# Another order of two transposings, and later places for small matmuls, in a two-branch mixer layer

## The chip, the cores and the metric

The kernel runs on one core of a Trainium2 chip. The metric is the device time of one execution in microseconds (us). TensorE does the matmuls, VectorE and ScalarE the elementwise work, GpSimd (Pool) the powers and some fills, and SyncE (SP) issues the DMAs. In the rows of the profile PE is TensorE's matmul, PEld its weight load, DVE is VectorE and ACT is ScalarE.

## The reference

Two layers run over 128 context tokens and 256 latent tokens, 384 rows of 2048 channels. In each, one input projection feeds two branches: A, a bidirectional RWKV-7 mixer with 16 heads of 64, and B, a bidirectional gated DeltaNet with 8 heads of 128 in chunks of 64 tokens. Both are projected back, merged by gates and projected once more. Of branch B this matters here:

```
lower = where(strict, einsum('nbhik,nbhjk->nbhij', kb, kc) * decay, 0)
t_inv = triangular_solve(eye + lower, eye, lower=True, unit_diagonal=True)
u  = t_inv @ (vc * beta)
wk = t_inv @ (kb * exp(gcum))
...                       # a scan over the chunks uses u, wk, q, k and the decays
```

Keys and queries are divided by their norms before, and the decays come from cumulative sums of g. Branch A has the same kind of inverse in its chunked form, and a norm of its own over k.

## The kernel before

The dense products (input projection, branch projections, merge, output projection) are streams of 128x128 weight tiles in float16, split from float32 on ScalarE (line 247) and VectorE (line 249) into a high and a low part; a product is 48 matmuls of 384 columns. They are one generator, `dense`. The branches are generators too, *threads*: `rwkv_front`, `rwkv_corner`, `rwkv_back` and `rwkv_out` for a pair of A's heads, `gdn_front`, `gdn_corner`, `gdn_scan` and `gdn_out` for a head of B (`gdn_corner` for two heads). `weave` sets TensorE's order once, when the program is written: it keeps a planned time, `now`, that each matmul advances. A thread yields either a number, the planned nanoseconds after which it wants to go on, or the name of an event that another thread sets. Whenever no thread is due, the products go on by one step (`STEP`, two tiles of the contraction, six matmuls). So the number that a thread yields between two matmuls says how much of the products TensorE gets to do between them. TensorE then keeps that order; it does not go past an instruction that waits. The other engines' orders are fixed as well, by a scheduler that works from the same program.

`HOP` (1100) is the allowance for one trip over another engine and back, `HOP_G` (4.4 of these) for a trip over VectorE, Pool and back, and `INVERT_A` and `INVERT_B` are those for an inverse in the two branches.

A head of branch B goes as follows. `gdn_front` builds `E` on VectorE, sums it by three matmuls with triangles (the decays), and takes the exponentials on ScalarE. It squares the keys (line 1280) and the queries (1290) on ScalarE and sums each by matmuls with `ones`; Pool takes the power (1299), and a matmul spreads the norms `rs`. The products of keys with keys and queries (`KQ`) follow, and VectorE and ScalarE write the masked, negated blocks into `nB`. After every second head `invert` inverts all 32x32 diagonal blocks of both heads on VectorE: a transposing into `ivw` (line 569), 30 steps of a multiply (574) and an add (576), and two transposings, `a1` in place of `nB` (580) and `a2` into the tile `iva` (581). `gdn_corner` waits for the event of the inverse, scales `a1` and `a2` into `Uf` on ScalarE (1351), and multiplies the corner block: a first product of `Ln` with `a2` (12 matmuls for a head, `tps<-iva,Ln` in the rows), a copy into `xc`, and a second product with `a1`. Then `gdn_scan` runs over the chunks. *Corner 1* to *corner 4* are the four pairs of heads in layer 0, *corner 5* to *corner 8* those in layer 1. Branch A's corners use the same `invert` (its results there are `nA` and `iva`) and also begin with `a2`.

At the start of branch B the products are held until head 0's front is done: the projections of head 2 wait for that event, and nothing else is left.

Of the kernel before, what the change touches and what calls it, by code (L numbers as in the profile page):

```python
# [27 lines left out]


HOP_G = 4.4  # L30
HOP, HOP_V, EVAC, CONV, DECAY, FIRST_B, INVERT_A, INVERT_B = 1100, 1.2, 2000, 8000, 7000, 3000, 37000, 48000

RANKS, STEP = (2000, 1000, 0, 0, 0, 0), 2

# [19 lines left out]
def backbone(ctx: ExitStack, tc: tile.TileContext, i, o):  # L54
    nc = tc.nc
    V, S, G, PE = nc.vector, nc.scalar, nc.gpsimd, nc.tensor
# [172 lines left out]
    def run(fast):  # L229
# [213 lines left out]
        def layer(l, par, cw, hpar, omka, xs, ready, next_start, after):  # L443
# [121 lines left out]
            def invert(pool, n_t):  # L565


                W = pool.tile([128, 32, 32], F32, tag="ivw", name="ivw", bufs=1)
                V.transpose(out=W, in_=n_t.rearrange("p b t -> p t b"))  # L569
                for j in range(1, 31):  # L570
                    n = 31 - j
                    tmp = pool.tile([128, 256], F32, tag="ivt", name="ivt", bufs=1)
                    tv = tmp[:, 0:n * j].rearrange("p (a b) -> p a b", b=j)
                    V.tensor_tensor(out=tv, in0=W[:, j + 1:32, j:j + 1].to_broadcast([128, n, j]),  # L574
                                    in1=W[:, j:j + 1, 0:j].to_broadcast([128, n, j]), op=MULT)
                    V.tensor_tensor(out=W[:, j + 1:32, 0:j], in0=W[:, j + 1:32, 0:j], in1=tv, op=ADD)  # L576
                G.memset(W.rearrange("p a b -> p (a b)")[:, 0:1024:33], 1.0)
                a1 = n_t
                a2 = pool.tile([128, 32, 32], F32, tag="iva", name="iva2", bufs=1)
                V.transpose(out=a1.rearrange("p b t -> p t b"), in_=W)  # L580
                V.transpose(out=a2.rearrange("p b s -> p s b"), in_=W.rearrange("p t s -> p s t"))  # L581
                return a1, a2


# [22 lines left out]
            for n in range(6):  # L607
                t = P.tile([128, 128], F32, tag=f"sring{n}", name=f"sring{n}", bufs=1)
# [37 lines left out]
            def rwkv_front(hp):  # L646
# [4 lines left out]
                k = act["k", hp]  # L651
                sq = P.tile([128, T], F32, tag="pe", name="sq", bufs=1)
                S.activation(out=sq, in_=k, func=AF.Square, scale=pcol(R_KK, hp))
                yield HOP
                t = tps()
                for b in range(NBLK):
                    mm(t[:, 2 * b:2 * b + 2], sq[:, 128 * b:128 * b + 128], bones[:, 0:128:64])
# [3 lines left out]
                t = tps()  # L661
# [12 lines left out]
                for d in range(2):  # L674
                    t = tps()
# [3 lines left out]
                    t = tps()  # L679
# [35 lines left out]
                    if d == 0:  # L715
                        yield "v", l, hp
                        v = act["v", hp]
                        t = tps()
# [16 lines left out]
                    for h in range(2):  # L735
                        for p in range(2):
                            t = tps()
# [10 lines left out]
                    for p in range(2):  # L748
                        t = tps()
# [8 lines left out]
                    t = tps()  # L758
# [488 lines left out]
            def gdn_front(h):  # L1247
# [11 lines left out]
                for n, (bm, d) in enumerate((("le", 0), ("lt", 1), ("ge", 1))):  # L1259
                    V.tensor_tensor(out=E[:, 3 * n:3 * n + 3, :], in0=half[bm].unsqueeze(1).to_broadcast([128, 3, 64]),  # L1260
                                    in1=bc(g[:, 8 * d + h, :], 64), op=MULT)
                yield 2 * HOP
                t = tps()
                mm(t[:, 0:192], tri["gt"], E[:, 0:3, :])
                mm(t[:, 192:384], tri["ge"], E[:, 3:6, :])
# [12 lines left out]
                ka = act["kb", h]  # L1278
                sq = Q.tile([128, T], F32, tag="th", name="sq", bufs=1)
                S.activation(out=sq, in_=ka, func=AF.Square)  # L1280
                yield HOP
                t = tps()
                for b in range(NBLK):
                    mm(t[:, b:b + 1], sq[:, 128 * b:128 * b + 128], ones[:, 0:1])
# [4 lines left out]
                sq = Q.tile([128, T], F32, tag="th", name="sq", bufs=1)  # L1289
                S.activation(out=sq, in_=qa, func=AF.Square)  # L1290
                S.copy(KQ[:, :, 1:3, :], c4(qa))
                yield HOP
                t = tps()
                for c in range(6):
                    b, p = divmod(c, 2)
# [1 line left out]
                with tc.high_priority(offset=1):  # L1297
                    V.tensor_scalar(out=rs[:, 3:6], in0=t[:, 0:3], scalar1=128.0, scalar2=128.0 * EPS, op0=MULT, op1=ADD)
                    G.tensor_tensor(out=rs, in0=rs, in1=mhalf[:, 0:6], op=ALU.pow)
                yield HOP_G * HOP  # L1300
                t = tps()
                for b in range(NBLK):
                    mm(t[:, 128 * b:128 * b + 128], rs[:, b:b + 1].to_broadcast([128, 128]), ident)
# [38 lines left out]
            def gdn_corner(h0):  # L1342
                yield "inverse", l, 8 + h0 // 2
                a1, a2 = act["inverse", h0 // 2]
                for hh in range(2):
                    Ln = act["front", h0 + hh][6]
                    i0 = 6 * hh
                    Uf = Q.tile([128, 2, NBLK, 64], F32, tag="Uf", name="Uf", bufs=4)
                    for q in range(2):
                        for d, a in ((0, a1), (1, a2)):  # L1350
                            S.mul(Uf[:, d, :, 32 * q:32 * q + 32], a[:, i0 + 3 * d:i0 + 3 * d + 3, :], m01[:, q:q + 1])
                    xc = Q.tile([128, 6, 32], F32, tag="xc", name="xc", bufs=2)
                    qs = [(slice(64 * p, 64 * p + 32), slice(64 * p + 32, 64 * p + 64)) for p in range(2)]
                    t = tps()
                    for n in range(6):
                        for q0, q1 in qs:
                            mm(t[q1, 32 * n:32 * n + 32], Ln[q0, n // 3, n % 3, 32:64], a2[q0, i0 + n, :])
                    for q0, q1 in qs:
                        S.copy(xc[q1].rearrange("p b c -> p (b c)"), t[q1, 0:192])
                    yield HOP  # L1360
                    t = tps()
                    for b in range(NBLK):
                        for q0, q1 in qs:
                            mm(t[q0, 32 * b:32 * b + 32], xc[q1, b, :], a1[q1, i0 + b, :])
                            mm(t[q1, 32 * b:32 * b + 32], a1[q1, i0 + 3 + b, :], xc[q1, 3 + b, :])
                    for q0, q1 in qs:
                        S.mul(Uf[q0, 0, :, 32:64], t[q0, 0:96].rearrange("p (b c) -> p b c", b=NBLK), -1.0)
                        S.mul(Uf[q1, 1, :, 0:32], t[q1, 0:96].rearrange("p (b c) -> p b c", b=NBLK), -1.0)
                    act["corner", h0 + hh] = Uf
                event(("corner", l, 8 + h0 // 2), HOP)  # L1370
# [178 lines left out]
    with tc.tile_pool(name="ck", bufs=1) as ck:  # L1549
# [14 lines left out]
        t = tps()  # L1564
# [33 lines left out]
```

## Time and profile before

| | |
|---|---|
| three runs, median | 3184.18 us (3180.49 to 3192.88) |
| the profiled execution | 3183.25 us, span 3180.3 us |
| granted TensorE clock, mean | 0.974 |
| TensorE matmul busy | 2991.0 us, 94% |
| TensorE weight loads | 1997.2 us, 63% |
| VectorE busy | 2310.9 us, 73% |
| ScalarE busy | 1455.9 us, 46% |

The span is what the profiler saw between the first and last instruction. Busy time is the sum of an engine's instructions over the whole span; branch A of layer 0 runs from some 140 to 950 us and its branch B to some 1460 us, those of layer 1 from 1670 to 2505 and to 2990 us. Granted clock is the share of TensorE's full clock: 1.0 is 2.4 GHz, 0.5 is 1.2 GHz, and there is no other level in the rows.

### The profile page before, as it was taken

What the parts mean: (1) busy time and instruction counts of PE and PEld (TensorE: products, weight loads), DVE (VectorE), ACT (ScalarE), POOL (GpSimd) and SP (SyncE); (2) the same over time, 40 slices, a digit from 0 to 9 for tenths busy, and PEclk for the clock granted to TensorE, in tenths of its full rate; (3) what the DMA queues carried; (4) which work ended last, traced back from release to release, by engine and by line L of the source; (5) the groups of instructions that cost most, each with busy time, mean ns of one, the idle gap of its engine ahead of it and who ended that gap; (6) DMA issues with size and microseconds to landing.
All of it is one profiled execution on the core that took longest, in us unless ns stands there. A gap on an engine that the chain in (4) does not pass through costs nothing. (4 is left out here: it accounts for less than half of the span.)

```text
span 3180.3 us, 69999 instructions
## 1 busy us (share of the span) xinstructions
PE 2991.0 (94%) x28531; PEld 1997.2 (63%) x28531; DVE 2310.9 (73%) x5968; ACT 1455.9 (46%) x3122; POOL 144.9 (5%) x198
## 2 busy tenths in 40 slices
PE   6899999999999999998979999999999998899898
PEld 2466666666665555555976666666666655565588
DVE  3268888888877777866354788888888678867744
ACT  3344444444434565453355444444443446564432
POOL 1000000011000000000000000000000000000000
PEclk8999999999999999999989999999999999999999
DMA  9854454454455436367455544433434442325655
GB/s 331 274 157 134 130 146 126 129 139 129 136 158 167 127 94 178 109 192 241 125 158 158 144 141 131 137 82 92 108 103 128 120 110 78 106 79 160 203 142 158
DMA packets 644359, 457.86 MB, mean 144 GB/s; under 512 B 28026, under 2 KB 611004, under 8 KB 642492
## 3 DMA queue, kind: packets, MB, share of 16 engines
q1 hardware_dynamic: 644028, 453.29, 49.1%
q8 instruction: 226, 3.70, 0.5%
q14 instruction: 105, 0.86, 0.1%
HBM read 421.74 MB, written 31.49 MB: 143 GB/s over the span
## 5 line engine op out<-in xcount | busy, mean ns | idle before, releaser
L95 PE MATMUL jps<-x,w 128*128 128x384 f16 x8640 | 1532.1, 330 | 10.1 <-ACT x L247 8.5
L95 PEld LDWEIGHTS <-w 128*128 128x128 f16 (+1 forms) x10368 | 975.9, 99 | 692.4 <-issue 100.6
L249 DVE SCALAR_TENSOR_TENSOR w<-st,w 128x1024 f16<-128x1024 f32 (+2 forms) x552 | 641.1, 1168 | 246.8 <-ACT w L247 241.9
L247 ACT ACTIVATE w<-st 128x1024 f16<-128x1024 f32 (+2 forms) x552 | 553.3, 1009 | 467.7 <-PE jps L95 304.5
L95 PE MATMUL cps<-w,mg 128*128 128x128 f16 x4608 | 263.6, 221 | 8.6 <-ACT mg L247 5.2
L95 PEld LDWEIGHTS <-mg 128*128 128x128 f16 x4608 | 262.0, 99 | 10.2 <-ACT mg L247 5.5
L576 DVE TENSOR_TENSOR ivw<-ivw,ivt 128x30 f32<-128x30 f32 (+4 forms) x720 | 236.6, 329 | 14.1
L574 DVE TENSOR_TENSOR ivt<-ivw 128x30 f32<-128x30 f32 (+4 forms) x720 | 236.6, 329 | 13.9
L95 PE MATMUL jps<-ya,w 128*128 128x384 f16 x768 | 137.7, 329 | 8.3 <-DVE z L562 2.9
L95 PEld LDWEIGHTS <-x 128*128 128x128 f16 x2304 | 132.3, 99 | 11.1 <-issue 7.9
L95 PE MATMUL jps<-w,x 128*128 128x128 f16 x2304 | 136.6, 220 | 0.0
L95 PE MATMUL tps<-AR,BK 64*128 64x128 f32 x768 | 121.6, 293 | 4.1 <-DVE GR L744 2.3
L95 PE MATMUL acc<-wm,cpad 128*32 128x256 f32 (+1 forms) x1664 | 112.0, 379 | 12.8 <-DMA wm<-in_w_mod 12.8
L757 ACT ACTIVATE nA<-GA 32x192 f32<-32x192 f32 x128 | 46.1, 360 | 152.7 <-DVE GA L742 151.7
L1400 ACT ACTIVATE os<-cps,gx 64x128 f32<-64x128 f32 x160 | 57.9, 362 | 117.6 <-DVE rt L1398 115.2
L95 PEld LDWEIGHTS tps<-AR,BK 64*128 64x128 f32 x768 | 97.0, 191 | 18.7 <-issue 4.3
L894 ACT COPY AR<-cps 64x128 f32<-64x128 f32 x192 | 49.5, 258 | 118.6 <-PE cps L95 104.9
L867 DVE COPY Z<-cps 64x128 f32<-64x128 f32 x192 | 55.4, 289 | 64.5 <-PE cps L95 60.8
L884 DVE SCALAR_TENSOR_TENSOR sring<-cps,pl,sp 64x64 f32<-64x64 f32 x256 | 72.5, 283 | 30.8 <-PE cps L95 26.5
L95 PEld LDWEIGHTS acc<-wm,cpad 128*32 128x32 f32 x1664 | 42.6, 110 | 61.4 <-issue 29.7
L1061 DVE TENSOR_TENSOR og<-cps,gp 128x128 f32<-128x128 f32 x96 | 27.6, 288 | 69.0 <-ACT junk L1060 69.0
L95 PE MATMUL jps<-yb,w 128*128 128x384 f16 x408 | 74.6, 329 | 1.4 <-ACT yb L247 1.3
(356 smaller groups left out, 3665.0 us busy)
## 6 DMA issues: line engine op xcount, KB each, us to landing
st<-in_w_in SPq DMA_DIRECT2D x194, 1024.0 KB
wm<-in_w_mod SPq DMA_DIRECT2D x176, 512.0 KB
st<-in_w_o SPq DMA_DIRECT2D x32, 1024.0 KB
st<-in_w_pa SPq DMA_DIRECT2D x32, 512.0 KB
gates<-gt SPq DMA_DIRECT2D x64, 192.0 KB
ms<-gates SPq DMA_DIRECT2D x32, 384.0 KB
st<-in_w_pb SPq DMA_DIRECT2D x11, 1024.0 KB
wm<-in_w_mod SPq DMA_DIRECT2D x32, 256.0 KB
```

Of the source, the lines that this page charges most:

```text
L95: PE.matmul(out, lhsT=lhsT, rhs=rhs, start=start, stop=stop, **kw)
L247: S.activation(out=dst[0], in_=src, func=AF.Copy, scale=scale)
L249: V.scalar_tensor_tensor(out=dst[1], in0=src, scalar=scale, in1=dst[0], op0=MULT, op1=SUB, accum_out=flag())
L574: V.tensor_tensor(out=tv, in0=W[:, j + 1:32, j:j + 1].to_broadcast([128, n, j]), in1=W[:, j:j + 1, 0:j].to_broadcast([128, n, j]), op=MULT)
L576: V.tensor_tensor(out=W[:, j + 1:32, 0:j], in0=W[:, j + 1:32, 0:j], in1=tv, op=ADD)
L757: S.mul(nA[rq, 6 * d:6 * d + 6, :].rearrange("p (h b) t -> p h b t", h=2), GA[rq, :, p, :, 32 * q:32 * q + 32], -1.0)
L867: V.tensor_copy(dirs[d][4][ar, b, p, :], pb[ar, 0:128])
L884: V.scalar_tensor_tensor(out=sn[hs, hs], in0=pb[hs, o0:o0 + 64], scalar=plc[hs], in1=sp[hs, hs], op0=MULT, op1=ADD)
L894: S.copy(AR[rr, b, 2 * p:2 * p + 2, :].rearrange("p a b -> p (a b)"), pas[d][rr, 0:128])
L1061: V.tensor_tensor(out=og[:, b, 128 * d:128 * d + 128], in0=t[:, 0:128], in1=gp[:, stream_of(b), 128 * d:128 * d + 128], op=MULT)
L1400: S.activation(out=os_[d][R_, b, :], in_=pas[d][R_, 0:128], func=AF.Copy, scale=egs[R_, x, b:b + 1])
```

## The change

In `invert` the two transposings change places: `a2`, which the corner's first product reads, is written first, `a1` second. `gdn_corner` scales `a2`'s half first. Five allowances grow: the inverse of branch B from 48000 to 52500, the squares of both branches (one in A, two in B) from 1 to 2.5 `HOP`, the norms of branch B from 4.4 to 6, and the decays from 2 to 3.5.

```diff
-HOP, HOP_V, ..., INVERT_A, INVERT_B = 1100, 1.2, ..., 37000, 48000
+HOP, HOP_V, ..., INVERT_A, INVERT_B = 1100, 1.2, ..., 37000, 52500
+HOP_S, HOP_N = 2.5, 6.0
...                                       invert
+V.transpose(out=a2.rearrange("p b s -> p s b"), in_=W.rearrange("p t s -> p s t"))
 V.transpose(out=a1.rearrange("p b t -> p t b"), in_=W)
-V.transpose(out=a2.rearrange("p b s -> p s b"), in_=W.rearrange("p t s -> p s t"))
...                                       rwkv_front, after the square of k
-yield HOP
+yield HOP_S * HOP
...                                       gdn_front, after E
-yield 2 * HOP
+yield 3.5 * HOP
...                                       gdn_front, after the squares of k and of q
-yield HOP
+yield HOP_S * HOP
...                                       gdn_front, after the power
-yield HOP_G * HOP
+yield HOP_N * HOP
...                                       gdn_corner
-for d, a in ((0, a1), (1, a2)):
+for d, a in ((1, a2), (0, a1)):
```

The changed file has two lines more at its head, so its line 97 is line 95 of before. Three places show what moves. First TensorE at a square of branch A, in layer 0 before head pair 4 (`w` are the parts of a weight tile, `x` of the input, and `bones` sums the squares); before:

```order
L95 LDWEIGHTS w_5546
L95 MATMUL jps<-x_198,w_5546 128x384
L95 MATMUL tps<-bones,sq 128x2 x3
L95 LDWEIGHTS w_5545
L95 MATMUL jps<-x_198,w_5545 128x384
```

and after:

```order
L97 MATMUL jps<-x_199,w_5545 128x384
L97 LDWEIGHTS w_5546
L97 MATMUL jps<-x_198,w_5546 128x384
L97 MATMUL tps<-bones,sq 128x2 x3
L97 LDWEIGHTS w_5545
L97 MATMUL jps<-x_198,w_5545 128x384
```

The three matmuls stand twelve rows later, behind six more products; so do all 16 squares of branch A. Second TensorE at the start of branch B in layer 1, where the products run out (`E` are the decays' sums, `sq` the squares of keys and queries, `rs` the norms, `p` the keys and values that are transposed); before:

```order
L95 LDWEIGHTS w_30107
L95 MATMUL jps<-x_19599,w_30107 128x384
L95 MATMUL tps<-ones,sq 128x1 x3
L95 MATMUL tps<-ones,sq 64x1 x6
L95 MATMUL tps<-ident,rs 128x128 x3
L104 MATMUL tps<-ident,p_29892 128x128 x3
L104 MATMUL tps<-ident,p_29658 128x128 x3
L95 MATMUL tps<-KQ 64x128 x6
```

and after:

```order
L97 LDWEIGHTS w_30107
L97 MATMUL jps<-x_19599,w_30107 128x384
L97 MATMUL tps<-E,m_gt 128x192
L97 MATMUL tps<-E,m_ge 128x192
L97 MATMUL tps<-E,m_lt 128x192
L97 MATMUL tps<-ones,sq 128x1 x3
L97 MATMUL tps<-ones,sq 64x1 x6
L97 MATMUL tps<-ident,rs 128x128 x3
L106 MATMUL tps<-ident,p_29892 128x128 x3
L106 MATMUL tps<-ident,p_29658 128x128 x3
L97 MATMUL tps<-KQ 64x128 x6
```

The last step of products has moved from behind the decays to ahead of them. Third VectorE at the end of corner 2's inverse (`ss` and `os` belong to a scan's output, `rt` to a scan's step, `vb` to the values); before:

```order
L574 TENSOR_TENSOR ivt<-ivw 128x30
L1314 TENSOR_TENSOR vb<-vtok,beta 128x384
L576 TENSOR_TENSOR ivw<-ivw,ivt 128x30
L1260 TENSOR_TENSOR E<-b_ge,g 128x192
L1398 SCALAR_TENSOR_TENSOR rt<-cps,neg,vtok 64x128
L1398 SCALAR_TENSOR_TENSOR rt<-cps,neg,vb 64x128
L580 STREAM_TRANSPOSE nB<-ivw 128x32x32
L581 STREAM_TRANSPOSE iva_12502<-ivw 128x32x32
```

and after:

```order
L576 TENSOR_TENSOR ivt<-ivw 128x30
L1262 TENSOR_TENSOR E<-b_le,g 128x192
L1457 TENSOR_TENSOR ss<-ss,rs 128x3
L578 TENSOR_TENSOR ivw<-ivw,ivt 128x30
L1262 TENSOR_TENSOR E<-b_lt,g 128x192
L193 TENSOR_SCALAR ss<-ss 128x3
L582 STREAM_TRANSPOSE iva_12635<-ivw 128x32x32
L1459 TENSOR_TENSOR ss<-ss,rs 128x3
L583 STREAM_TRANSPOSE nB<-ivw 128x32x32
```

The two transposings have changed places, and other small work stands around them, since VectorE's order was made anew.

## Rows read from the trace of the kernel before

**Rows 1.** The page's busy times of each engine.

```profile
PE 2991.0 (94%) x28531; PEld 1997.2 (63%) x28531; DVE 2310.9 (73%) x5968; ACT 1455.9 (46%) x3122; POOL 144.9 (5%) x198
```

**Rows 2.** TensorE's waits: engine, tile, line, releaser: us in total, times, longest.

```profile
PE tps L95 <- DVE iva L581: 20.6, 7, 5.6
...
PE tps L95 <- POOL rs L1299: 7.2, 3, 3.4
...
PE tps L95 <- ACT sq L653: 6.7, 6, 1.9
...
PE tps L95 <- ACT sq L1280: 4.8, 3, 2.0
...
PE tps L95 <- ACT E L1268: 3.0, 2, 1.6
PE tps L95 <- DVE kk L666: 2.9, 2, 2.6
```

**Rows 3.** TensorE's timeline at corners 2, 3, 6, 7: start, length, operation [idle before].

```profile
1124.21 0.85 PE L95 MATMUL tps<-iva,Ln 32*32 32x32 f32 x24 [4.49 <-DVE iva L581]
...
1223.65 0.57 PE L95 MATMUL tps<-iva,Ln 32*32 32x32 f32 x24 [4.53 <-DVE iva L581]
...
2683.41 0.85 PE L95 MATMUL tps<-iva,Ln 32*32 32x32 f32 x24 [5.62 <-DVE iva L581]
...
2782.17 0.85 PE L95 MATMUL tps<-iva,Ln 32*32 32x32 f32 x24 [4.80 <-DVE iva L581]
```

**Rows 4.** VectorE's timeline, the first transposing of the same four inverses.

```profile
1068.10 1.94 DVE L569 STREAM_TRANSPOSE ivw<-nB 128x1024 f32<-128x1024 f32 x1
...
1173.92 1.98 DVE L569 STREAM_TRANSPOSE ivw<-nB 128x1024 f32<-128x1024 f32 x1
...
2627.18 1.95 DVE L569 STREAM_TRANSPOSE ivw<-nB 128x1024 f32<-128x1024 f32 x1
...
2727.62 1.97 DVE L569 STREAM_TRANSPOSE ivw<-nB 128x1024 f32<-128x1024 f32 x1
```

**Rows 5.** Busy us by stretch: PE, PEld, DVE, ACT, POOL, then clock, DMA.

```profile
1068.00:1124.00 56.00, 47.51 (x355) 28.75 (x353) 52.34 (x152) 29.48 (x75) 2.40 (x3) 0.98 0.42 120
1174.00:1224.00 50.00, 45.29 (x336) 26.30 (x336) 47.49 (x135) 22.71 (x57) 1.01 (x2) 1.00 0.51 155
2627.00:2683.00 56.00, 47.04 (x324) 28.91 (x322) 52.56 (x152) 31.83 (x78) 2.41 (x3) 0.99 0.31 82
2728.00:2782.00 54.00, 47.81 (x315) 27.59 (x313) 51.22 (x150) 26.81 (x72) 1.85 (x3) 0.99 0.47 130
...
1318.00:1353.00 35.00, 33.20 (x215) 19.51 (x213) 33.39 (x89) 8.61 (x18) 0.15 (x1) 1.00 0.27 81
```

**Rows 6.** VectorE's groups, whole span: count | busy us, mean ns of one | idle before.

```profile
L249 DVE SCALAR_TENSOR_TENSOR w<-st,w 128x1024 f16<-128x1024 f32 (+2 forms) x552 | 641.1, 1168 | 246.8 <-ACT w L247 241.9 <-PE cps L95 3.6
...
L574 DVE TENSOR_TENSOR ivt<-ivw 128x30 f32<-128x30 f32 (+4 forms) x720 | 236.6, 329 | 13.9
...
L581 DVE STREAM_TRANSPOSE iva<-ivw 128x1024 f32<-128x1024 f32 x24 | 48.0, 2000 | 0.0
...
L1196 DVE SCALAR_TENSOR_TENSOR p<-jps,cw,p 128x127 f32<-128x127 f32 x96 | 39.3, 409 | 5.7 <-ACT p L1194 5.2
```

**Rows 7.** The same view as rows 5, behind a square of branch A, layer 0.

```profile
497.40:500.80 3.40, 3.40 (x14) 2.04 (x14) 3.33 (x10) 0.00 (x0) 1.01 (x1) 0.50 0.69 239
```

**Rows 8.** TensorE's timeline at the norm of head 1, layer 1.

```profile
2559.85 1.65 PE L95 MATMUL tps<-ident,rs 128*128 128x128 f32 x6 [3.35 <-POOL rs L1299]
2561.29 4.05 PE L95 MATMUL jps<-x,w 128*128 128x384 f16 x12
...
2565.77 2.15 PE L95 MATMUL jps<-x,w 128*128 128x384 f16 x12
```

**Rows 9.** Corner 8: VectorE's last transposing and TensorE's first matmuls, timeline.

```profile
2895.39 2.01 DVE L581 STREAM_TRANSPOSE iva<-ivw 128x1024 f32<-128x1024 f32 x1
...
2902.42 0.57 PE L95 MATMUL tps<-iva,Ln 32*32 32x32 f32 x24
```

More of the change, by code (lines that the diff above doesn't have):

```diff
@@ L30 @@
 HOP_G = 4.4
-HOP, HOP_V, EVAC, CONV, DECAY, FIRST_B, INVERT_A, INVERT_B = 1100, 1.2, 2000, 8000, 7000, 3000, 37000, 48000
+HOP, HOP_V, EVAC, CONV, DECAY, FIRST_B, INVERT_A, INVERT_B = 1100, 1.2, 2000, 8000, 7000, 3000, 37000, 52500
+HOP_S, HOP_N = 2.5, 6.0
 RANKS, STEP = (2000, 1000, 0, 0, 0, 0), 2
@@ L1291, in gdn_front @@
                 S.copy(KQ[:, :, 1:3, :], c4(qa))
-                yield HOP
+                yield HOP_S * HOP
                 t = tps()
```

## The prediction

> **What bounds the kernel now.** Start with the page's line of busy times: TensorE's matmuls fill 94% of the span, VectorE 73% [rows 1]. The list of whom TensorE waited for then gives the waits that this change aims at: 20.6 us for the second transposing of the inverse (line 581), 6.7 us for branch A's squares (653), 4.8 us for branch B's key squares (1280), 7.2 us for its norms (1299) and 3.0 us around its decays (1268) [rows 2]. Together that is 42 us, 1.3% of the span, and TensorE idles in all of it, since its order is fixed and nothing can overtake the waiting matmul. So the first question is whether the waits go away, or only move.
>
> For that, read where they lie. Four of branch B's eight corners wait, 4.49, 4.53, 5.62 and 4.80 us, always for line 581; the other four find their inverse done [rows 3]. Their inverses had begun at 1068.10, 1173.92, 2627.18 and 2727.62 [rows 4], so they took 50 to 56 us from the first transposing to the corner. In such a stretch VectorE is busy for 93 to 95% of the time, 52.34 of 56, 47.49 of 50, 52.56 of 56 and 51.22 of 54 us [rows 5]. This is the important thing in the profile: inside these stretches VectorE, not TensorE, sets the end, although over the span TensorE does. An inverse's end is then the sum of what stands in VectorE's fixed order between its first and last transposing, and TensorE's wait is what it has too little of.
>
> **The corners, the largest term.** Two edits meet there. The allowance of 52,500 for 48,000 puts 21 to 26 more matmuls between the last keys and the corner, mostly products of 384 columns (281 to 307 matmuls for corner 2, 282 to 303 for corner 3, 277 to 303 for 6 and 7). Twelve such matmuls take 2.15 us [rows 8], some 0.17 us each with the last one's drain left out, so this fills 4.4, 3.6, 4.4 and 4.4 us. The swap lets the first product, which reads only the second result, begin one transposing of 2.0 us earlier [rows 6]. But the new order also puts other work on VectorE between the inverse's first transposing and that result, and with VectorE full that work counts. In corner 2's stretch stand two more weight splits (1.17 us each) and five more convolution steps (some 0.4 us each) against five scan and decay steps fewer [rows 6]: with the 2.0 us that have moved behind, +1.7 us. In the same way corner 3 gets -2.8 us, corner 6 -0.2 us and corner 7 +2.2 us. All are scaled by 0.94, since the rows of a stretch sum to 59.6 us where 56.0 us passed (they overlap a little).
>
> Corner 2: of the 56.1 us from 1068.10 to 1124.21, TensorE waited 4.49 us at the corner and some 3.5 us earlier in the same stretch (half of the 3.0 us of decays and one of the three key squares, 2.0 us) [rows 2, 3, 4]. That leaves 48.1 us of work, 52.5 us after; VectorE needs 57.6 us. The waits fall from 8.0 to 5.1 us: 2.9 us gained. The earlier ones are not gained on top, since TensorE would only reach the corner sooner. Corner 3: 49.7 us with 4.53 us of waits, 45.2 us of work, 48.8 after; VectorE 47.1: nothing is left to wait for, 4.5 us. Corner 6: 56.2 us with 9.1 us of waits (the other half and another square), 47.1 of work, 51.5 after; VectorE 56.0: 4.6 us. Corner 7: 54.6 us, waits 4.8, 49.8 of work, 54.2 after; VectorE 56.6: 2.4 us. Sum 14.4 us. Bounds: 4.5 us if only corner 3 gains, and 19.4 us with the 7 us of earlier waits if VectorE keeps up.
>
> **Head 1 of layer 1** waits 3.35 us for its norm [rows 8], ahead of a corner that does not wait; the allowance of 6 for 4.4 moves two more steps of products in front of it, 12 matmuls, 2.0 us gained. A key square of 0.9 us outside the stretches goes as well: 2.9 us. The other two norm waits (7.2 less 3.35 us) stand at the start of branch B, where the products are held until head 0's front is done, and no order can fill them: nothing. In layer 1 one step of six products now stands ahead of the decays there instead of behind them, so less lies between: a loss of up to 1.0 us, counted whole.
>
> **Branch A** (16 heads) moves each square's sum by exactly one step of six products, 1.0 us. Six waits sum to 6.7 us, the longest 1.9 [rows 2]; 1.0 us or the whole of each goes: 4.7 us. Its own corners' three short waits for line 581 (20.6 less 19.4 us) go by the swap: 1.1 us. The norm's product moves by the same step, but at five of the 16 heads the low-rank product behind it does not, so 1.0 us less stands between them. Where little stood there already, one wait for kk was 2.6 us and one 0.3 us [rows 2]; I take the small end at five places, 1.5 us lost (ends 0 and 13). Branch A gains 4.3 us.
>
> **The clock.** After a longer wait TensorE runs at the lower of its two levels (1.2 instead of 2.4 GHz): granted 0.50 from 497.4 to 500.8 [rows 7], behind one of the two squares that wait 1.9 us; and behind the norm of head 1, 12 products take 4.05 us instead of 2.15 [rows 8]. What a removed wait gives back is thus more than itself. In branch A two such stretches go (1.4 us each, some nine products at 0.16 us more); of corner 3's 1.0; of the norm's some 3 us (1.9 of it in those 12 products) I count half, since 1.35 us of wait remain; and 1.0 for the shorter waits of 2, 6 and 7. Sum 6.3 us (ends 3 and 14).
>
> **What the change adds.** ScalarE's four scalings of a head's blocks now meet the second transposing's result 2 us after the first's; the copies behind the first product are queued behind them, and the second product needs both copies and result. The last of these is ready no later than before, while the first product is out sooner, so nothing is lost against before, but in the three full stretches 0.3 us each may show: 1.0 us. Counted in matmuls, the scans of heads 0 to 5 move 8 to 22 us later among the products and the last pair's 1 to 2 us earlier, so by the order the end of branch B does not move. But the last inverses share VectorE with more of these scans: 6.7 us more rows in layer 0 and 1.7 in layer 1, in a stretch already at 33.39 of 35 us [rows 5]. The corner itself has room: corner 8's result is there at 2897.4, and its matmuls begin at 2902.42 [rows 9]. The products' evacuations inside the stretch have none; I take 3 us (ends 0 and 8.4). DMA issues change places on SP as well, weight loads with gate stores; two staging buffers cover that, and in branch B TensorE waited for no weights' DMA: nothing, and at most a wait of some us if that cover went. Pool's powers stay where they were.
>
> **Sum.** 14.4 + 2.9 + 4.3 + 6.3 - 1.0 - 1.0 - 3.0 = 22.9 us against the profiled 3183.3 us, which stands 0.9 us under the median of the three runs: 3161 us on the median's side.
>
> **Rivals.** (a) *VectorE takes it back.* With the longer stretches VectorE's fixed order gets worse than by my count and the three full corners wait as long as before: 9.9 us of the corners' 14.4 and 3 us of clock are gone, leaving 10 us, and up to 4 more in new short waits: 3175 to 3178. For it speaks the share of 95%; against it, that the allowance gives TensorE 4 us more to do in each stretch, and that it is VectorE's row counts that gave me no more than 14 us. The Trainium skill states this as a rule (Perfetto Trace Analysis, Identifying the Most-Contended Engine): the engine to relieve is the one with the highest occupancy, and TensorE's matmul share does not count, its weight loads do. By that rule VectorE (73%) stands above TensorE's loads (63%) [rows 1], an edit that only re-orders TensorE would bring little, and the time would be this rival's; the trace agrees inside the inverses' stretches and not outside them.
> (b) *All waits go.* The inverses end sooner, because what TensorE no longer waits for also arrives sooner at VectorE: 19.4 + 7 + 2.9 + 5.8 + 13 of clock less 2 = 46 us, 3138 us. Against it: sums of rows, not arrival, set VectorE's ends there.
> (c) *Slower.* The moved scans run into the last pair's inverses. A scan has six steps with some six VectorE operations each, and if each of these queues behind one inverse step of 0.33 us [rows 6], a head's scan takes 12 us longer. For two heads in layer 0 and one in layer 1 that is 36 us, and as the last scans come behind these on the same thread, the end of branch B moves with them: 13 us over before, 3196 us. It decides when VectorE falls behind by more than corner 8 has to spare: the 5.0 us of [rows 9] and the 4 us of added products, 9 us against the 1.7 that I count.
>
> **How the numbers follow.** Half a per cent, 16 us, is about what a measurement of this kernel can tell from no change. My forecast 0.46 (3153 to 3168), (a) 0.28, (b) 0.16, (c) 0.10. Faster: forecast 0.44 and (b) 0.16, 0.60 together; same: (a), the forecast's edge and the part of (c) that ends within half a per cent, 0.32; slower: the rest of (c), 0.08. The range must leave out at most 2 in 10: (c) and half of (b) stay outside, 3140 to 3181.
>
> **What would show it.** After the change the wait for the inverse at corner 3 should be gone, and at corners 2, 6 and 7 still 2 to 6 us; the key squares and decays ahead of them should wait no more. VectorE should read 93% or more in the same stretches. Branch A's waits for squares should sum to 2 us or less and the low level behind them be gone; the norm of head 1 in layer 1 should wait 1 to 2 us. Corners 2, 6 and 7 without wait would be (b); unchanged waits with a span over 3170, (a); long waits between the last two corners' fronts and the end of branch B, (c). I am wrong at the root if the waits vanish and the span does not follow: then TensorE is not what the time hangs on outside these stretches.

## The result, and the profile after

The changed kernel is slower: 3205.01 us median (3201.45 to 3213.58) against 3184.53 us (3180.49 to 3192.88), four runs each, ratio 1.0072 with a 95% interval of 1.0055 to 1.0090. Forecast were 3161 us and a range of 3140 to 3181. The profiled span went from 3180.3 to 3199.7 us. The page's busy line of after, beside [rows 1], splits these 19.4 us:

```profile
PE 2999.8 (94%) x28531; PEld 2002.8 (63%) x28531; DVE 2314.1 (72%) x5968; ACT 1459.3 (46%) x3122; POOL 133.6 (4%) x198
```

The same 28,531 matmuls take 8.8 us longer (2999.8 for 2991.0; the mean granted clock is 0.969 for 0.974), and TensorE idles 10.6 us more (199.9 for 189.3). The list of TensorE's waits (tile, line, releaser: us in total, times, longest) shows where. Lines of after stand two higher than before's:

```profile
PE tps L97 <- DVE kk L668: 22.3, 8, 3.7
PE tps L97 <- POOL rs L1301: 13.2, 5, 3.4
PE tps L106 <- DVE p L1306: 12.6, 5, 5.5
PE cps L97 <- DVE Z L869: 9.1, 3, 4.4
...
PE tps L97 <- ACT u L680: 4.7, 7, 0.7
PE tps L97 <- ACT Uf L1370: 4.3, 2, 3.1
...
PE tps L106 <- ACT Uf L1370: 3.2, 2, 2.2
...
PE tps L97 <- DVE iva L582: 3.0, 1, 3.0
...
PE tps L97 <- ACT sq L655: 1.8, 2, 0.9
```

Beside [rows 2], what the change aimed at did go: line 581's 20.6 us are 3.0 (line 582), branch A's squares 6.7 us are 1.8, and branch B's key squares have left the list. But five waits grew. VectorE's kk was 2.9 us in two and is 22.3 in eight, the Z product of branch A 3.7 and is 9.1, branch B's norm (rs) 7.2 and is 13.2, the transposing of the normalised key (p, line 1306) had no wait before and has 12.6 (before's one wait for a p, 1.5 us, is for a value's, line 1200), and the waits for Uf, 7.5 in all, are new. So the profile already names two questions: what happened at kk in branch A, and where branch B's corner waits went.

**Branch A.** Take one pair of heads, the fifth of layer 0, on TensorE (start, length, operation, count, [idle before and releaser]). Before:

```profile
413.10 0.88 PE L95 MATMUL tps<-ident,rs 128*64 128x128 f32 x12 [0.24 <-POOL rs L192]
413.91 0.91 PE L95 MATMUL tps<-lo,wup 96*128 96x384 f32 x2
415.49 0.91 PE L95 MATMUL tps<-lo,wup 96*128 96x384 f32 x2 [0.67 <-ACT u L678]
```

and after:

```profile
411.60 0.88 PE L97 MATMUL tps<-ident,rs 128*64 128x128 f32 x12
412.41 0.91 PE L97 MATMUL tps<-lo,wup 96*128 96x384 f32 x2
416.89 0.97 PE L97 MATMUL tps<-lo,wup 96*128 96x384 f32 x1 [3.57 <-DVE kk L668]
```

The first row is the norm's product, the next two the first pair of low-rank products (lines 676 and 680). VectorE reads the norm's product to make kk. Its row for that, first of before, then of after:

```profile
418.24 0.61 DVE L666 SCALAR_TENSOR_TENSOR kk<-k,par,tps 128x384 f32<-128x384 f32 x1
```

```profile
416.23 0.61 DVE L668 SCALAR_TENSOR_TENSOR kk<-k,par,tps 128x384 f32<-128x384 f32 x1
```

VectorE is no later than before: 4.26 us behind the norm's product before (418.24 against 413.98), 3.75 after (416.23 against 412.48). Yet before, the third product ran at 415.49, almost 3 us ahead of kk, and waited 0.67 us for ScalarE alone; after, it stands still until VectorE has read. No data go from kk to the low-rank product. What they can share is the buffer. `tps()` takes from a pool of two PSUM banks, the buffers that matmuls write to and other engines read from. The norm's product holds one, the first low-rank product takes the other, and the second gets, by the addresses in the program, either the bank that ScalarE empties at once or the bank that waits for VectorE. It is the latter for 2 of the 16 pairs before and for 9 after. The scheduler chose it when the program was written. The trace bears the count out: at nine pairs of after the second low-rank product starts 0.05 or 0.06 us behind the end of kk (416.89 against 416.84 above), and at the other seven it runs 3 to 6 us ahead of that end. The Trainium skill describes the symptom (Perfetto Trace Analysis, Optimization Strategy): the same gap repeating on the engine that should be full can mean too few buffers in SBUF or PSUM; the trace agrees, with eight waits of up to 3.7 us. Behind this wait TensorE also ran at its lower level, 1.2 GHz; these are windows of after and of before from that product's start (busy of PE, PEld, DVE, ACT, POOL, then the granted clock and the DMA's share and rate):

```profile
416.89:420.00 3.11, 3.11 (x18) 2.32 (x19) 2.79 (x9) 1.42 (x3) 0.00 (x0) 0.51 1.06 271
```

```profile
415.49:420.00 4.51, 4.51 (x70) 4.15 (x71) 4.47 (x11) 1.08 (x2) 0.00 (x0) 1.00 0.48 153
```

**Branch B.** At corners 2, 3, 6 and 7 TensorE's timeline of after shows, beside the 4.49, 4.53, 5.62 and 4.80 us of [rows 3]:

```profile
1154.87 0.57 PE L97 MATMUL tps<-iva,Ln 32*32 32x32 f32 x24 [1.30 <-DVE ss L1459]
...
1245.30 0.57 PE L97 MATMUL tps<-iva,Ln 32*32 32x32 f32 x24
...
2722.39 0.57 PE L97 MATMUL tps<-iva,Ln 32*32 32x32 f32 x24
...
2822.52 0.85 PE L97 MATMUL tps<-iva,Ln 32*32 32x32 f32 x24 [2.96 <-DVE iva L582]
```

But from the inverse's first transposing to the corner it is now 60.9, 51.6, 65.7 and 61.6 us where it was 56.1, 49.7, 56.2 and 54.6. More products stand in there, which is only a move, and new waits do too. In corner 6's stretch the waits are in front of the next head's norm and of the transposing of its key (TensorE):

```profile
2699.94 1.19 PE L97 MATMUL tps<-ident,rs 128*128 128x128 f32 x6 [2.94 <-POOL rs L1301]
2702.41 0.90 PE L106 MATMUL tps<-ident,p 128*128 128x128 f32 x3
...
2710.58 0.87 PE L106 MATMUL tps<-ident,p 128*128 128x128 f32 x3 [5.50 <-DVE p L1306]
```

and VectorE's timeline between them:

```profile
2701.89 0.61 DVE L1437 SCALAR_TENSOR_TENSOR S<-S,gx,cps 128x128 f32<-128x128 f32 x2 [2.12 <-PE cps L97]
...
2704.89 0.36 DVE L1400 SCALAR_TENSOR_TENSOR rt<-cps,neg,vtok 64x128 f32<-64x128 f32 x1 [1.13 <-PE cps L97]
...
2706.44 1.21 DVE L251 SCALAR_TENSOR_TENSOR w<-st,w 128x1024 f16<-128x1024 f32 x1
...
2709.89 0.54 DVE L1306 TENSOR_TENSOR p<-p,tps 128x384 f32<-128x384 f32 x1
```

The norm's product was out at 2701.13; VectorE multiplied the key by it only at 2709.89, behind scan steps, weight splits and steps of the inverse. And VectorE itself stood still for 2.12 and 1.13 us, for products that TensorE had not reached because it was waiting for the norm. The two engines wait for each other in turn. The windows from first transposing to corner show it for the four stretches, beside the 93 to 95% of [rows 5]:

```profile
1093.94:1154.87 60.93, 55.40 (x384) 32.37 (x382) 53.22 (x160) 33.77 (x84) 4.02 (x4) 0.94 0.34 98
1193.75:1245.30 51.55, 50.13 (x362) 28.51 (x360) 48.98 (x141) 27.42 (x73) 1.07 (x2) 1.00 0.60 179
2656.72:2722.39 65.67, 56.09 (x364) 33.23 (x362) 56.79 (x163) 36.92 (x93) 3.24 (x4) 0.92 0.23 61
2760.95:2822.52 61.57, 54.34 (x363) 32.50 (x362) 56.25 (x163) 34.75 (x83) 3.30 (x4) 0.95 0.40 109
```

VectorE reads 87, 95, 86 and 91%: only corner 3's stretch is as full as before.

Behind the four corners stand the new waits for Uf. The longest on TensorE, and ScalarE's row that ends it:

```profile
1251.99 0.83 PE L97 MATMUL tps<-ones,sq 128*128 128x1 f32 x6 [3.10 <-ACT Uf L1370]
```

```profile
1251.69 0.24 ACT L1370 ACTIVATE Uf<-tps 32x96 f32<-32x96 f32 x1
```

Uf is what ScalarE copies out of the corner's second product. The sums of the key squares read nothing of it, yet begin some 0.05 us behind its end; so do the other three, two transposings of a scan's output and the next head's corner product. All take their bank from the pool of two, so by the timing this is branch A's wait for a bank once more, though no run here took these products out of that pool. ScalarE came to this Uf only at 1250.93, behind a key square and a weight split, while the product was out at 1248.6.

### The profile page after: what moved, and what is told of

It reads as the page before. It is cut to its first block, busy times and chain, and to the rows that moved or that the text cites. A ratio compares the mean times of both kernels' runs of the same rounds, so it can differ in the third digit from the quotient of the medians.

```text
span 3199.7 us, 70022 instructions
## 1 busy us (share of the span) xinstructions
PE 2999.8 (94%) x28531; PEld 2002.8 (63%) x28531; DVE 2314.1 (72%) x5968; ACT 1459.3 (46%) x3122; POOL 133.6 (4%) x198
## 5 line engine op out<-in xcount | busy, mean ns | idle before, releaser
L896 ACT COPY AR<-cps 64x128 f32<-64x128 f32 x192 | 49.7, 259 | 124.3 <-PE cps L97 110.7
L97 PE MATMUL tps<-lo,wup 96*128 96x384 f32 x128 | 59.6, 572 | 27.0 <-DVE kk L668 22.3
```

What stands on the lines that cost most here:

```text
L97: PE.matmul(out, lhsT=lhsT, rhs=rhs, start=start, stop=stop, **kw)
L896: S.copy(AR[rr, b, 2 * p:2 * p + 2, :].rearrange("p a b -> p (a b)"), pas[d][rr, 0:128])
```

## The experiments

Each ratio is against runs of the kernel before on the same chip (before's medians there: 3185.1, 3184.7, 3183.5 and 3185.3 us). *A* and *B* are parts of the profiled span: B from branch B's first decay product to its last `swp,os` transposing, both layers; A all else up to layer 1's branch B, without the 40 us of products between branch B's end and the output product in layer 0. *Shared banks* are the pairs of branch A (of 16) whose second low-rank product gets the bank of the norm's product, by the addresses in the program. *A* and *B* come from one profiled execution each: the nine kernels with 2 shared banks, whose branch A is the same but for the swap in its inverse, read 1967.1 to 1978.1 for A.

| kernel | median us | ratio, 95% interval | shared banks | A us | B us |
|---|---|---|---|---|---|
| before | 3184.5 | 1 | 2 | 1968.3 | 978.9 |
| after | 3205.0 | 1.0072 (1.0055 to 1.0090) | 9 | 1988.5 | 981.3 |
| a_square_only | 3204.8 | 1.0067 (1.0055 to 1.0080) | 9 | 1982.3 | 981.1 |
| all_but_a_square | 3187.6 | 1.0017 (1.0006 to 1.0029) | 2 | 1971.7 | 983.7 |
| after_kk_cps | 3178.1 | 0.9975 (0.9962 to 0.9987) | 0 | 1957.6 | 985.8 |
| after_kk_prio | 3218.3 | 1.0110 (1.0095 to 1.0124) | 12 | 2003.0 | 980.7 |
| before_kk_cps | 3179.3 | 0.9986 (0.9977 to 0.9995) | 0 | 1957.8 | 979.2 |
| square_kk_cps | 3176.3 | 0.9978 (0.9968 to 0.9988) | 0 | 1959.0 | 980.7 |
| swap_only | 3183.7 | 0.9997 (0.9985 to 1.0009) | 2 | 1974.3 | 978.6 |
| inv_only | 3175.4 | 0.9970 (0.9959 to 0.9981) | 2 | 1971.0 | 970.2 |
| b_steps_only | 3189.5 | 1.0018 (1.0008 to 1.0029) | 2 | 1968.6 | 984.0 |
| norm_only | 3200.6 | 1.0047 (1.0033 to 1.0061) | 2 | 1978.1 | 997.5 |
| swap_inv | 3174.1 | 0.9967 (0.9954 to 0.9980) | 2 | 1970.2 | 972.3 |
| swap_inv_norm | 3184.2 | 1.0000 (0.9986 to 1.0013) | 2 | 1967.1 | 983.3 |
| swap_inv_squares | 3175.6 | 0.9971 (0.9958 to 0.9983) | 2 | 1974.6 | 971.4 |
| inv_square_kk_cps | 3168.8 | 0.9952 (0.9938 to 0.9966) | 0 | 1958.1 | 973.1 |
| swap_inv_kk_cps | 3166.3 | 0.9946 (0.9927 to 0.9965) | 0 | 1960.4 | 970.6 |

**Branch A.** First the square's step alone, on the kernel before:

```diff
                 S.activation(out=sq, in_=k, func=AF.Square, scale=pcol(R_KK, hp))
-                yield HOP
+                yield 2.5 * HOP
```

> The kernel before with one edit alone: branch A's squares get 2.5 allowances instead of 1. Theory 1 (the PSUM bank): the second low-rank product of a head pair is given the bank from which VectorE still has to read kk, at 9 of the 16 pairs instead of 2, and TensorE waits for kk there. It expects nearly the whole loss: waits for kk of 18 to 23 us in total (2.9 us before) and 3198 to 3206 us. Theory 2 (branch B's later scans cost the time, the squares gain as I forecast): waits for squares down by 4.7 us and 3177 to 3182 us.

Its waits:

```profile
PE tps L95 <- DVE kk L666: 22.3, 8, 3.7
PE tps L95 <- DVE iva L581: 19.4, 4, 5.6
PE cps L95 <- DVE Z L867: 8.5, 3, 4.2
...
PE tps L95 <- ACT sq L653: 1.8, 2, 0.9
```

One number in one line gives the whole loss, with branch B's corners untouched. The same 22.3 us in eight waits stand at kk. The changed kernel with this line alone put back (`HOP`):

> The changed kernel with branch A's squares back at one allowance; the swap and all of branch B's allowances stay. Theory 1: kk's waits are back at some 3 us, branch A as before, and only branch B's stages differ: 3182 to 3192 us. Theory 2: the loss lies in branch B and stays, 3203 to 3210 us.

It is 0.17% over the kernel before, and the waits for kk are 2.9 us again. That leaves the cause of the waits. In after_kk_cps the changed kernel takes the norm's product from the pool of three banks, and in after_kk_prio VectorE's instruction is put ahead:

```diff
-                t = tps()
+                t = cps()
                 for b in range(NBLK):
                     for h in range(2):
                         mm(t[64 * h:64 * h + 64, 128 * b:128 * b + 128], rs
...
```

> The changed kernel with one edit: the norm's product of branch A, from which kk is read, is put into the pool of three banks that the scans use, not into the pool of two that the low-rank products use. Nothing else is changed. Theory 1: no low-rank product can meet kk's bank, waits for kk fall to 0 to 1 us, 3183 to 3192 us, up to 8 us more if the scans now wait for a third bank. Theory 2: no change, 3203 to 3207 us.

```diff
-                V.scalar_tensor_tensor(out=kk, in0=k, scalar=pcol(R_KK, hp), in1=t[:, 0:T], op0=MULT, op1=MULT)
+                with tc.high_priority(offset=2000):
+                    V.scalar_tensor_tensor(out=kk, in0=k, scalar=pcol(R_KK, hp), in1=t[:, 0:T], op0=MULT, op1=MULT)
```

> The changed kernel with one edit: VectorE's multiplication for kk is put ahead of the inverse's steps and weight splits in VectorE's order (a higher priority). The bank of the second low-rank product is still kk's, at 12 of 16 pairs by the program. Theory 1 in the form that the wait is VectorE's lag (3 to 4 us from the norm's product to kk) times the shared bank: with the lag gone the waits fall to under 1 us each, 5 to 8 us in total, 3185 to 3195 us. If sharing a bank costs by itself, whatever the lag: waits as now or more, 3203 to 3212 us. Theory 2: 3203 to 3207 us.

With the third bank no wait for kk is left, nor for u, and the changed kernel falls below the one before, 5 us under the range that I had given theory 1. The higher priority did not do what I expected: at eight of the nine pairs that shared the bank VectorE came no earlier, at the ninth 0.3 us, at three others it came 1.4 to 2.0 us earlier, and the new order put these three on the shared bank as well, 12 in all. Its row:

```profile
PE tps L97 <- DVE kk L669: 32.7, 11, 4.4
```

This unplanned dose tells the most: pairs on the shared bank 0, 2, 9, 12; waits for kk 0, 2.9, 22.3, 32.7 us; A's time 1957.6, 1971.7, 1988.5, 2003.0 us (after_kk_cps, all_but_a_square, after, after_kk_prio). Whether an earlier VectorE alone would have shortened the waits stays untested. Is the square's step worth anything once the bank is out of the way? The kernel before with the pool edit alone, and with pool and square:

> The kernel before, with the norm's product of branch A from the pool of three banks. This is the other half of square_kk_cps (3176 us). If the squares' step is worth what the prediction gave it (4.7 us of waits and some 3 us of clock), this kernel is at 3182 to 3186: waits for kk (2.9 us) gone, waits for squares still 6.7 us. If instead the pool alone made that gain, it is at 3175 to 3179.

> The kernel before with two edits in branch A alone: the step behind the key square 2.5 for 1 (as in a_square_only, 3205 us), and the norm's product taken from the pool of three banks instead of the pool of two that the low-rank products use. Theory 1 (the whole loss of a_square_only is the low-rank product that gets the bank that VectorE still reads): the waits for kk of 22.3 us go to 0, the waits for squares fall from 6.7 to under 2 us as in the changed kernel, and the time is 3174 to 3181, under the kernel before. Rival (VectorE is late with kk for another reason, and who reads it, the k.q products, waits instead; or the three-bank pool's own users wait): a wait of 10 us or more appears at those products or at the Z product, and the time is 3190 to 3205.

Waits of before_kk_cps, then of square_kk_cps:

```profile
PE tps L95 <- ACT sq L653: 6.7, 6, 1.9
...
PE cps L95 <- DVE Z L867: 5.4, 3, 2.6
```

```profile
PE cps L95 <- DVE Z L867: 10.4, 3, 5.1
...
PE tps L95 <- ACT sq L653: 1.8, 2, 0.9
```

The 4.9 us of squares have moved to the Z product: it waits 8.5 to 10.8 us in all six kernels with the square's step and 3.7 to 7.6 in the eleven others. 0.9986 and 0.9978 overlap, and A took 1957.8 and 1959.0 us. At 3179.3 us the pool alone lies between my two expectations, nearer the one by which it makes the gain; the square's step is worth nothing that these runs can tell.

**Branch B, edit by edit.** The swap alone:

```diff
-                V.transpose(out=a1.rearrange("p b t -> p t b"), in_=W)
                 V.transpose(out=a2.rearrange("p b s -> p s b"), in_=W.rearrange("p t s -> p s t"))
+                V.transpose(out=a1.rearrange("p b t -> p t b"), in_=W)
...
-                        for d, a in ((0, a1), (1, a2)):
+                        for d, a in ((1, a2), (0, a1)):
```

> Only branch B's swap (second result transposed and multiplied first), on the kernel before. Theory 1 (an inverse in a full stretch ends when VectorE's row is done; the swap lets TensorE begin the corner one transposing of 2.0 us earlier): each of the four waiting corners keeps a wait of 2 to 3.5 us instead of 4.5 to 5.6, in sum 8 to 13 us where it was 19.4, branch A's waits for kk stay at 2.9 us, and the time falls by 4 to 9 us, to 3176 to 3181. Theory 2 (VectorE's total sets the end of a stretch, whatever is begun first): the corner waits fall by the same amount but come back at the norm, E or key-square matmuls of the same stretches, and the time stays within 3 us of 3185.

```profile
PE tps L95 <- DVE iva L580: 12.5, 4, 3.9
...
PE tps L95 <- ACT sq L1280: 8.0, 4, 3.2
```

The corners gave up 6.9 us as the first theory said, and the time did not move, as the second said. In B, 3.2 us came back at the squares, TensorE's idle time fell by 4.3 us (65.8 to 61.5), and its busy time rose by 4.0 (913.1 to 917.1), so the clock took what was left; the last section shows where. Outside B, Z waits 2.2 us more and the output product, where it first reads the merged rows (`mg`), 3.0 more; but these two are at least as long in inv_only, which is 9 us faster than before. The allowance alone:

```diff
-HOP, HOP_V, EVAC, CONV, DECAY, FIRST_B, INVERT_A, INVERT_B = 1100, 1.2, 2000, 8000, 7000, 3000, 37000, 48000
+HOP, HOP_V, EVAC, CONV, DECAY, FIRST_B, INVERT_A, INVERT_B = 1100, 1.2, 2000, 8000, 7000, 3000, 37000, 52500
```

> Only the inverse's allowance in branch B, 52,500 for 48,000, on the kernel before: more products stand ahead of each corner, nothing else moves. Theory 1: TensorE has some 4 us more to do ahead of the four waiting corners; their waits fall from 19.4 us to 8 or less, and the time falls by 6 to 12 us, to 3173 to 3179. Theory 2 (VectorE-bound stretch): the corner's wait falls, but the products behind it are fewer and the next head's norm and squares wait by as much; time 3183 to 3188.

```profile
PE tps L95 <- POOL rs L1299: 16.6, 5, 5.5
...
PE tps L95 <- DVE iva L581: 8.5, 6, 5.4
```

A gain of 9 us. Here too 9.4 us came back at the norm (7.2 to 16.6), but the corners gave 12 and the squares and decays some 6.7. The three smaller allowances:

```diff
-                yield 2 * HOP
+                yield 3.5 * HOP
...
-                yield HOP
+                yield 2.5 * HOP
...
-                yield HOP
+                yield 2.5 * HOP
...
-                yield HOP_G * HOP
+                yield 6 * HOP
```

> Only branch B's three smaller allowances (decays 3.5 for 2 steps, key and query squares 2.5 for 1, norm 6 for 4.4), on the kernel before: no swap, the inverse's allowance as before. Theory 1 (waits are filled one by one): the waits for E and the key squares (7.8 us) and 2 us of the norm's go, nothing comes back; time 3174 to 3179. Theory 2 (in a stretch that VectorE fills, an earlier wait that is filled comes back at the corner or at the next norm): the corner's waits grow by 3 to 8 us from 19.4 us, and the time is 3183 to 3192.

```profile
PE tps L95 <- DVE iva L581: 18.9, 7, 11.1
PE tps L104 <- DVE p L1304: 16.6, 6, 5.0
```

The time is theory 2's, the place is not: the four corners wait no more than before in sum (17.8 us for 19.4), corners 2, 3 and 6 less (2.18, 2.52 and 1.97 us) and corner 7 more (11.13). What came back stands mostly at the transposing of the normalised key, 16.6 us. The last of the three allowances alone (6 for `HOP_G`, 4.4):

> Only branch B's norm allowance, 6 steps for 4.4, on the kernel before. Theory 1 (the norm's product moves back, the transposes that read the key which VectorE has normalised do not move with it, so the lead of VectorE's multiplication shrinks): the waits of those transposes (tps<-ident,p for line 1304) are 10 us or more, most of the 16.6 us in b_steps_only, waits for the norm fall below 5 us, and the time is 3186 to 3192, all of what b_steps_only lost. Rival (the decays and squares of b_steps_only made the loss): such waits are under 5 us and the time is 3180 to 3185.

The time went against me in size (+17 us, more than all three together), and the mechanism that I named is not it: the waits at p are 2.2 us. Two of its rows for waits, and a window from first transposing to corner 2:

```profile
PE tps L95 <- ACT sq L1280: 9.4, 4, 3.1
PE tps L95 <- POOL rs L1299: 8.5, 4, 3.5
```

```profile
1079.14:1141.53 62.39, 52.02 (x350) 30.46 (x348) 53.75 (x154) 31.80 (x79) 2.40 (x3) 0.91 0.32 91
```

The norm waits no less than before, the squares 4.6 us more, VectorE's share in the stretch is 86%, and the clock 0.91 where it was 0.98 [rows 5]. Then both large edits, and on top of them the norm, or decays and squares:

> Branch B's swap and the inverse's allowance of 52,500 together, on the kernel before. Apart they gave -1 and -9 us. If edits add up: 3172 to 3178, with the four corners' waits in sum under 5 us. If the stretches are VectorE's and the corner's room is used up by the allowance already (corner 3 waits no more, corner 2 for 1.5 us): the swap adds nothing or costs, since in its order VectorE does other work ahead of the second result: 3175 to 3184, with waits for norms of 14 us or more as in inv_only (16.6).

> swap_inv (3174 us) and branch B's norm allowance of 6 steps for 4.4, nothing else. Theory N (the norm's edit alone takes the gain back): 3185 to 3195, TensorE's waits at the transposes of the normalised key 8 us or more, at the norm no less than the 17 us of swap_inv. Theory S (the allowances for decays and squares do it): 3171 to 3178, transposes under 4 us, the norm's waits down to 10 us or less.

> swap_inv (3174 us) and branch B's allowances for decays (3.5 for 2) and for key and query squares (2.5 for 1), the norm's left at 4.4. Theory N: 3170 to 3177, waits at the transposes under 4 us. Theory S (these edits push the whole chain of a head's front, norm included, against the transposes that do not move): 3182 to 3190, waits at the transposes 8 us or more.

Waits of swap_inv, of swap_inv_norm and of swap_inv_squares:

```profile
PE tps L95 <- POOL rs L1299: 16.9, 5, 5.5
```

```profile
PE tps L95 <- POOL rs L1299: 9.4, 4, 4.5
```

```profile
PE tps L95 <- POOL rs L1299: 14.9, 8, 4.8
```

By the times theory N holds, at the edge of its range: the norm's edit takes the 9 us back (0.9967 to 1.0000, intervals apart; 3184.2 us where 3185 to 3195 was expected), decays and squares do not (0.9971). By the waits it holds in part: the norm's waits fell by 7.5 us, where none less was expected, and the transposes of the key, in all, wait 4.8 us, not 8. The 12.6 us at p in the changed kernel need the norm's and the other steps together. Both large edits together give no more than the allowance alone.

**Versions meant to beat both.**

> A version meant to beat both kernels: the kernel before with the key square's step of branch A at 2.5, branch A's norm product from the pool of three banks, and the inverse's allowance of branch B at 52,500; no swap, branch B's other steps as before. If the two gains (8.3 us in branch A, 9.2 us in branch B) are of different places and add up: 3164 to 3171. If they share a cause (the clock, or the wait for weights at branch B's end, which takes back what comes earlier): 3171 to 3177.

> swap, the inverse's allowance of 52,500, and branch A's norm product from the pool of three banks; branch A's square step as before. If the square's step is worth what the prediction gave it, this is 3 to 6 us behind a kernel that has it too (inv_square_kk_cps, 3169 us): 3170 to 3176. If the low-rank product's bank was the whole matter and the Z product takes back what the squares no longer wait (5.4 us became 10.4 us), it is level with it or better: 3164 to 3170.

Both do, and they are level: the gains of the pool and of the allowance lie in different parts (A -8 to -10 us, B -6 to -8 us) and add up to 0.5%. The one without the square's step is no slower.

## Why the prediction was wrong

**The step that failed** is in *Branch A*: the norm's product moves, "at five of the 16 heads the low-rank product behind it does not, so 1.0 us less stands between them", and from there "the small end at five places, 1.5 us lost (ends 0 and 13)". The kind of place and the sign were right; the heads and the mechanism were not. At those five heads (in before the first low-rank product starts 1.0 us behind the norm's, in after at once) the lead did shrink and TensorE waits for kk at none of them: the second low-rank product runs 3 to 4 us ahead of kk's end. All eight waits stand at other heads. I counted products between the norm and the low-rank product, when the two are tied only by a bank, and whether they are tied at all hung on a choice that the same edit made anew. The two waits for kk in [rows 2] should have raised the question why the other 14 heads did not wait, though VectorE ended kk there 1.5 to 8.2 us behind the norm's product, at the two 1.1 and 3.4. The bank answers it, and the addresses in the program tell it before any run. Measured: kk 19.4 us more, of which 4.7 replace waits for u on the same products, so +14.7; and the upper end of 13 was too low as well.

**Branch A's squares** were right in size as waits (4.7 forecast, 4.9 measured), and worth nothing that the times show: Z took 5 us. I had not asked what is late next behind a square.

**The corners.** My sum was per stretch, so compare it per stretch, all waits of TensorE over 0.2 us from the last key products to the corner: 8.7, 4.5, 9.2 and 6.1 us before, 5.5, 1.2, 9.5 and 6.9 after. Corners 2 and 3 gained 3.2 and 3.3 us of a forecast 2.9 and 4.5; corners 6 and 7 lost 0.3 and 0.8 where I forecast gains of 4.6 and 2.4. So the step that failed is the same line of working for the last two: "47.1 of work, 51.5 after; VectorE 56.0". It lets nothing but VectorE's row count and the corner set the end, and has no term for a wait that the change brings into the stretch. Such waits came, 2.94 and 5.50 us in corner 6's, and because VectorE then stood still for TensorE, its 56.0 us became 59.3 to the second result, and TensorE reached the corner 6.3 us later still. Over the whole span the corners gave 14.0 us (19.4 to 5.4), and the transposes of the key took 12.6, the norms 6.0 and the waits for Uf 7.5; with what squares and decays gave beside the corners, TensorE's idle time in B is 65.8 us before and 65.9 after. The prediction's rival (a) describes this, with "up to 4 more in new short waits" where it was some 26; VectorE's share, 93% or more by the prediction, was 86 to 95%. The rule of the Trainium skill weighed there (Perfetto Trace Analysis, Identifying the Most-Contended Engine) ranks engines by occupancy, and TensorE by its share of the peak rate and its weight loads; that a new order on TensorE would bring little was the prediction's own step from it. That step fits branch B taken together, 978.9 to 981.3 us, and not its best edit: inv_only moves TensorE's work alone and won 9 us.

**Head 1 of layer 1.** Its norm wait of 3.35 us [rows 8] is gone, more than the 2.0 that I counted. In norm_only, where the same step moves alone, it is 1.17 us, but a new one of 3.49 ends at 2693.75.

**The clock** was counted at 6.3 us of gain, and TensorE's busy time rose by 8.8, some 2 of it in B. Long waits came in, not out, and behind the one shown above the level was low; that they make up the whole sum is not shown. **The losses that I added** do not fare alike. The copies at the corners, 1.0 us, were mis-sized: the waits for Uf are 7.5 us. They are 0.3 in swap_inv and 3.4 in swap_inv_squares, so they come with the moved steps and not with the swap alone. Layer 1's start, 1.0 us, lost nothing: TensorE's waits there are 4.3 us before and 4.4 after. The last inverses, 3.0 us, could not be told apart; corner 8 did not wait, and rival (c) did not happen. The slower side came from a mechanism that I had put among the bounds.

Open stays why the norm's later place costs 10 to 17 us. TensorE's idle and busy times both rise in B, by 6 and 13 us in the profile of norm_only, but no single wait carries it; and that profile is of its slowest run, 11 us over its median.

## What to carry to other kernels

When an edit moves a small matmul whose result a slow engine reads, ask which PSUM buffer the next products get and who empties it; in a pool of two, the order in which the program is scheduled decides that, and moving one number elsewhere can turn it. If some of many equal places wait and the others do not, find out why before pricing the edit. In a stretch that two engines share to 90%, count waits over the whole stretch up to the next point with slack: a filled wait is a gain only if nothing behind it is late by as much.

## What the chip showed beside that

The same waits need not cost the same clock. In swap_only, whose order on TensorE is that of before, the stretch has the same two waits as before, 1.64 us for E and 1.96 for the key square, and then (first before, then swap_only, from behind them to the corner's wait):

```profile
1105.00:1119.72 14.72, 14.72 (x120) 9.32 (x116) 13.79 (x49) 8.38 (x19) 1.48 (x2) 1.00 0.40 122
```

```profile
1109.50:1127.20 17.70, 17.70 (x130) 11.06 (x128) 14.38 (x50) 8.39 (x19) 1.48 (x2) 0.86 0.32 100
```

The granted clock is 1.00 (2.4 GHz) in one and 0.86 in the other. TensorE does not idle in either, yet the same 144 matmuls from the key squares to the corner's wait take 17.6 us in one and 20.6 in the other. These 3 us are about what the swap had won at corners 2 and 3 (1.8 and 1.7). So a forecast of what a removed wait gives back in clock is good to some us at best, and single profiles of one kernel differ by as much as these edits are worth (before_kk_cps: span 3169.3, median 3179.3); the table's verdicts go by the medians.
